# Two-layer hybrid diffusion backbone: GpSimd's low-part subtractions in parts of 256 columns

## The chip, the cores and the metric

The kernel runs on one core of a Trainium2 chip. The metric is the device time of one execution in microseconds (us). Before the change three runs gave a median of 2991.61 us (2990.83 to 2998.21).

## The reference

The input is a stream of 1024 latent tokens and 256 context tokens of width 1024, in float32. Two layers follow. Every sub-layer is modulated (a shift, a scale and a gate from a SiLU vector), and ends in a residual and a layer norm; each layer closes with a squared-ReLU MLP of inner width 4096.

```python
h  = x  * (1.0 + sc1)  + sh1          # modulated latents; context tokens alike (hc)
# layer 0: one projection feeds 4 retention heads and 4 gated-linear-attention heads,
# both bidirectional and chunked (64 tokens); context states start the latent scan
yc, ctx_states = retention_gla_mixer(hc, *prm, s0)
y, _ = retention_gla_mixer(h, *prm, ctx_states);  y = y @ ev_w_out
# layer 1: grouped-query attention, window +-128, a sink logit per head, axial rotary,
# latent queries also read all context keys
y = merge_heads(window_attention(q, k, v, k_c, v_c, sink)) @ od_w_out
x = layer_norm(ALPHA * x + g1 * y)                                  # both layers
x = layer_norm(ALPHA * x + g2 * (square(relu((x*(1+sc2)+sh2) @ w1)) @ w2))
```

## The kernel before, in words

**Three matmuls for one.** Every large product is made in a reduced float32 form (`F32R`). An operand is first cut in two: a high part, its rounded copy, and a low part, `operand - high`. Then `mm3` (L240 to L243) accumulates three matmuls per 128-deep step k in PSUM: weight high by activation high (L241), weight high by activation low (L242), weight low by activation high (L243). So each weight tile and each activation tile needs one copy and one subtraction.

**Who cuts the weights.** `wsplit` (L224) loads a weight tile of 128x1024 into one of three `raw` buffers, lets ScalarE copy the high part (L229) and lets one engine subtract the low part (L230). That engine is GpSimd unless the caller names another. 260 weight tiles pass through it; 210 subtractions are on GpSimd and 50 on VectorE. In the layer-0 mixer stage the generator `srcs` lets u odd go to VectorE and u even to GpSimd, and `wnext` holds three tiles ahead of the one in use. `load_wv` (L541) cuts eight value weights the same way, five of them on GpSimd (L546).

**Who cuts the activations.** `split` (L233) makes the high part on VectorE (L237) or ScalarE (L235), the low part (L238) on the engine that is named. `h_steps` (L345) works through the eight k of a modulated tile in pairs of 128x512 (two k of 256 tokens): ScalarE scales and shifts, then `split`, with the low part in turn on VectorE and on GpSimd. In the first stage the low part of the third token chunk (128x1024, two k of 512 tokens) is GpSimd's too. Two subtractions of the layer-0 mixer's outputs are written out by hand and do not go through `split`: L985 (eight on GpSimd, 128x1024) and L981 (two on GpSimd, 128x512).

**The stages in order of time.** First projections of layer 0 with their modulation (to about 165 us); the scan states (to about 350 us); the layer-0 mixer, five pairs of 128-token tiles, in which projections, the output projection and layer norms of neighbouring pairs are woven into the scan by credit (`slot`, to about 740 us); the MLP of layer 0 (to about 1690 us); the attention's projections (to about 1860 us); attention with its output projection (to about 2255 us); the MLP of layer 1. In the MLPs `load(b+1)` asks for four weight tiles one block ahead of their use, and the pool `wg` has five `w` buffers.

**What orders the work.** The code is written in the wanted order. A scheduler places each engine's instructions, tracks which columns of a tile an instruction writes and reads, and puts in the semaphore waits; each engine then runs its own queue strictly in that order. GpSimd's queue also carries the scaling at the end of each layer norm (`acc`, L714), a scaling of the gates (L807), small copies that release DMAs, and some DMA issues.

Other names in the text: VectorE (DVE) adds a projection's output to the residual at L734 (`w_out_steps`) and L1040 (MLP), masks the scores of the gated-linear heads into `Pg` at L928, multiplies the gate tile `g` at L978, keeps the scan states `S` at L898, L900 and L902, subtracts and scales in the layer norm at L690 and L708, and squares the ReLU output `r` at L1025. L943 is the TensorE matmul that reads `Pg`; L664 sums for a layer norm. L1193 transposes the rotated keys or queries `kr`, which L1187 writes.

Of the kernel before, what the change touches and what calls it, by code (L numbers as in the profile page):

```python
# [9 lines left out]
F32 = mybir.dt.float32  # L10
# [4 lines left out]
ALU = mybir.AluOpType  # L15
# [19 lines left out]
def backbone(ctx: ExitStack, tc: tile.TileContext, xT, cin, wmod, bmod, lng, lnb, w1, w2,  # L35
# [9 lines left out]
    V, S, G, TE, SY = nc.vector, nc.scalar, nc.gpsimd, nc.tensor, nc.sync  # L45
# [11 lines left out]
    def nm(s):  # L57
        uid[0] += 1
        return f"{s}_{uid[0]}"
# [164 lines left out]
    def wsplit(pool, src, eng=None):  # L224
        raw = rawp.tile([P, 1024], F32, tag="raw", name=nm("raw"))
        SY.dma_start(raw, src)
        both = pool.tile([P, 2, 1024], F32R, tag="w", name=nm("w"))
        hi, lo = both[:, 0, :], both[:, 1, :]
        S.copy(hi, raw)  # L229
        (eng or G).tensor_tensor(lo, raw, hi.bitcast(F32), ALU.subtract)  # L230
        return hi, lo

    def split(hi, lo, src, lo_eng=None, hi_eng=None):  # L233
        if hi_eng is S:
            S.copy(hi, src)  # L235
        else:
            V.tensor_copy(hi, src)  # L237
        (lo_eng or V).tensor_tensor(lo, src, hi.bitcast(F32), ALU.subtract)  # L238

    def mm3(pt, wh, wl, xh, xl, start, stop):  # L240
        TE.matmul(pt, lhsT=wh, rhs=xh, start=start, stop=False)  # L241
# [107 lines left out]
    def h_steps(src, l, idx, j, hh, hl, tp, tag, nb=1, hi_eng=None, los=(V, G)):  # L349

        n = src.shape[2]
        for k2 in range(KT // 2):
            tmp = tp.tile([P, 2, 256], F32, tag=tag, name=nm("hf"), bufs=nb)
            for i in range(2):
                k = 2 * k2 + i
                S.activation(tmp[:, i, :n], src[:, k, :], AF.Identity, scale=osc[:, l, idx, k, j:j + 1],
                             bias=mod[:, l, 3 * idx, k, j:j + 1])
            split(hh[:, 2 * k2:2 * k2 + 2, :], hl[:, 2 * k2:2 * k2 + 2, :], tmp[:, :, :n], los[k2 % 2], hi_eng)
            yield
# [3 lines left out]
    with es_b1:  # L363
# [6 lines left out]
        lwh = b1.tile([P, 256], F32R, tag="lwh", name="lwh")  # L370
        lwl = b1.tile([P, 256], F32R, tag="lwl", name="lwl")
        split(lwh, lwl, lw)
        w0 = wsplit(wp, wfm[0])
        pus, pls = [pX() for _ in range(3)], [pX(), pY(), pY()]

# [8 lines left out]
        for q in range(4):  # L384
            first_mods(q, raws)
            x_ = xs
            if q < 3:
                raws = first_load(q + 1)
                xs = first_x(q + 1)
            for a in range(2):  # L390
                k = 2 * q + a
                for j, c0, c1 in ((1, 0, 256), (0, 256, T)):
                    S.activation(x_[:, a, c0:c1], x_[:, a, c0:c1], AF.Identity, scale=osc[:, 0, 0, k, j:j + 1],
                                 bias=mod[:, 0, 0, k, j:j + 1])
            for ci, (c0, N) in enumerate(CH):
                split(h1[ci][0][:, 2 * q:2 * q + 2, :], h1[ci][1][:, 2 * q:2 * q + 2, :], x_[:, :, c0:c0 + N],
                      G if ci == 2 else V)
            if q > 0:
                first_proj(q - 1)
# [60 lines left out]
        def unit_loop(*uf):  # L460
            wus = [wsplit(wp, wfm[u]) for u, _ in uf]
            for ci in range(3) if len(uf) == 1 else (2, 1, 0):
                c0, N = CH[ci]
                for wu, (_, fn) in zip(wus, uf):
                    pt = pX()
                    proj(pt, wu, h1, ci)
                    fn(pt, ci, N, c0)
# [60 lines left out]
    with pool(name="b2", bufs=1) as b2:  # L528
# [11 lines left out]
        def load_wv(k):  # L540
            raw = rawp.tile([P, 1024], F32, tag="raw", name=nm("raw"))  # L541
            SY.dma_start(raw, wv[k])
            hi = b2.tile([P, 1024], F32R, tag=f"wvh{k}", name=f"wvh{k}")
            lo = b2.tile([P, 1024], F32R, tag=f"wvl{k}", name=f"wvl{k}")
            S.copy(hi, raw)
            (V if k > 2 and k % 2 else G).tensor_tensor(lo, raw, hi.bitcast(F32), ALU.subtract)  # L546
            wvh.append(hi)
            wvl.append(lo)

# [18 lines left out]
        for k in range(3):  # L568
            load_wv(k)
        x0 = load_x(0, 1)  # L570
        for k in range(3, KT):
            load_wv(k)
        Scur = new_S()
        G.memset(Scur[64:128, 1:3], 0.0)
        for oi, t in enumerate(order):
# [6 lines left out]
            for hf, k in [(hf, k) for k in range(KT) for hf in range(2)] if oi == 0 else [(hf, k) for hf in range(2) for k in range(KT)]:  # L582
                sl = slice(hf * 512, hf * 512 + 512)
# [140 lines left out]
    def w_out_steps(y, wsrc, wp, acc, l, j, pW, engs=(None, None), wnext=None):  # L724

        n = acc.shape[2]
        yh, yl = y
        for u in range(KT):
            wh, wl = [w.rearrange("p (k m) -> p k m", k=KT) for w in (wnext() if wnext else wsplit(wp, wsrc[u], engs[u % 2]))]
            pt = pW()  # L730
            for k in range(KT):
                xh, xl = [y_[k // 4][:, k % 4, :] if isinstance(y_, list) else y_[:, k, :] for y_ in (yh, yl)]
                mm3(pt[:, :n], wh[:, k, :], wl[:, k, :], xh, xl, k == 0, k == KT - 1)
            V.scalar_tensor_tensor(acc[:, u, :], pt[:, :n], gta[:, l, 0, u, j:j + 1], acc[:, u, :],  # L734
                                   op0=ALU.mult, op1=ALU.add)
            yield
# [15 lines left out]
    with pool(name="b3", bufs=1) as b3:  # L752
# [99 lines left out]
        for tp_ in range(NT // 2):  # L852
# [118 lines left out]
            for i in range(2):  # L971
                sl = slice(i * P, (i + 1) * P)
# [238 lines left out]
    for grp in range(3):  # L1211
# [19 lines left out]
        for i in range(4):  # L1231
            src = wkv[i] if grp == 0 else wq[4 * (grp - 1) + i]
            wu.append(wsplit(wg, src, V if i % 2 else G))
        for t in range(0 if grp == 0 else 2, NT):
# [14 lines left out]
            n = t - 2  # L1249
# [315 lines left out]
```

## Time and profile before

| | before |
|---|---|
| median of 3 runs | 2991.61 us |
| the profiled execution | 2999.63 us, span 2997.8 us |
| TensorE (PE) busy | 2886.7 us, 96% of the span |
| VectorE (DVE) busy | 1618.5 us, 54% |
| ScalarE (ACT) busy | 982.1 us, 33% |
| GpSimd (POOL) busy | 811.2 us, 27% |
| mean granted TensorE clock | 0.986 |

The profile names an instruction by its source line, engine and operation, then `out<-in` by tile names with buffer numbers left out. "x210" is a count. A group's row gives its busy time and the mean of one in ns, and behind the bar the idle time of the engine before these instructions with what released it. In the view of waits a row gives who waited for whom, the total in us, how often, and the longest. A row of the timeline gives the start in us, the duration in us (of all merged instructions where the count is over 1), and in brackets the idle time before it. A row of a source line gives minimum, median and maximum in ns. A stage's row gives busy time and counts per engine, then the granted TensorE clock.

### The profile page before, as it was taken

The numbers are of one execution on the slowest core, as the hardware profiler recorded it, in microseconds if no ns is written. First come the engines' busy times: TensorE is split into PE (matmuls) and PEld (weight loads), VectorE is DVE, ScalarE is ACT, GpSimd is POOL, SyncE is SP. The second block draws the span as 40 slices with busy tenths as digits, with TensorE's granted clock in tenths as the row PEclk, the third lists the DMA queues.
The fourth block names the chain that finished last, engine by engine and source line by source line (L and its number), as shares of the span: only waits on it lengthen the run. The fifth ranks groups of instructions, "written<-read, shape, count | busy, mean of one in ns | idle before, by whom it ended". The sixth has DMA issues, their size and how long they took to land. (4 is left out here: it accounts for less than half of the span.)

```text
span 2997.8 us, 42313 instructions
## 1 busy us (share of the span) xinstructions
PE 2886.7 (96%) x17204; PEld 2389.1 (80%) x17204; DVE 1618.5 (54%) x2709; ACT 982.1 (33%) x1630; POOL 811.2 (27%) x610
## 2 busy tenths in 40 slices
PE   7989998999999999999999999999999999999997
PEld 4866788888888888888888777677678888888886
DVE  3754467777765544444534554666775343433346
ACT  4533344443311111111112532656653111122113
POOL 3120144455311111111111432234343222122111
PEclk9999999999999999999999999999999999999999
DMA  7378576663122222122210385122221111111111
GB/s 256 113 224 251 179 245 202 204 204 124 55 69 71 71 70 71 57 74 85 67 43 8 97 214 162 45 80 89 64 86 42 57 57 44 41 57 56 36 36 57
DMA packets 168354, 304.45 MB, mean 102 GB/s; under 512 B 13504, under 2 KB 98752, under 8 KB 167648
## 3 DMA queue, kind: packets, MB, share of 16 engines
q1 hardware_dynamic: 149744, 272.91, 28.4%
q0 software_dynamic: 6480, 16.26, 2.0%
q10 hardware_dynamic: 11936, 12.59, 1.5%
q8 instruction: 135, 2.21, 0.3%
q14 instruction: 59, 0.48, 0.1%
HBM read 257.67 MB, written 44.04 MB: 101 GB/s over the span
## 5 line engine op out<-in xcount | busy, mean ns | idle before, releaser
L230 POOL TENSOR_TENSOR w<-raw,w 128x1024 fp32r<-128x1024 f32 x210 | 508.7, 2430 | 1644.5 <-ACT w L229 1602.4
L1040 DVE SCALAR_TENSOR_TENSOR acc<-k,gta,acc 128x512 f32<-128x512 f32 (+1 forms) x704 | 441.2, 648 | 567.4 <-PE k L243 559.9
L242 PE MATMUL k<-hl,w 128*128 128x256 f32 (+1 forms) x1632 | 554.5, 340 | 5.9 <-POOL hl L238 4.6
L241 PE MATMUL k<-hh,w 128*128 128x256 f32 (+1 forms) x1632 | 554.4, 340 | 5.1 <-DVE hh L237 3.4
L243 PE MATMUL k<-hh,w 128*128 128x256 f32 (+1 forms) x1632 | 551.1, 338 | 0.2 <-POOL w L230 0.2
L229 ACT CAST w<-raw 128x1024 fp32r<-128x1024 f32 x260 | 269.4, 1048 | 768.8 <-PE k L243 450.8
L241 PE MATMUL k<-uh,w 128*128 128x512 f32 (+1 forms) x1408 | 498.8, 354 | 9.2 <-DVE acc L1040 8.8
L242 PE MATMUL k<-ul,w 128*128 128x512 f32 (+1 forms) x1408 | 495.5, 352 | 0.0
L243 PE MATMUL k<-uh,w 128*128 128x512 f32 (+1 forms) x1408 | 494.7, 351 | 0.0
L241 PEld LDWEIGHTS k<-hh,w 128*128 128x128 f32 x1632 | 312.4, 192 | 49.9 <-issue 11.4
L242 PEld LDWEIGHTS k<-hl,w 128*128 128x128 f32 x1632 | 312.5, 192 | 45.5 <-POOL hl L238 6.1
L243 PEld LDWEIGHTS k<-hh,w 128*128 128x128 f32 x1632 | 312.9, 192 | 33.1 <-issue 1.7
L241 PEld LDWEIGHTS k<-uh,w 128*128 128x128 f32 x1408 | 266.9, 190 | 54.3 <-DVE acc L1040 16.6
L242 PEld LDWEIGHTS k<-ul,w 128*128 128x128 f32 x1408 | 266.9, 190 | 36.1 <-issue 0.8
L243 PEld LDWEIGHTS k<-uh,w 128*128 128x128 f32 x1408 | 266.8, 189 | 36.2 <-issue 0.8
L1022 ACT ACTIVATE r<-k 128x512 f32<-128x512 f32 (+1 forms) x176 | 90.6, 515 | 611.9 <-PE k L243 611.6
L241 PE MATMUL k<-yh,w 128*128 128x256 f32 (+1 forms) x544 | 183.7, 338 | 7.7 <-DVE acc L734 7.7
L159 DVE SCALAR_TENSOR_TENSOR k<-raw,cs,k 128x256 f32<-128x256 f32 (+1 forms) x168 | 96.5, 575 | 161.4 <-DMA raw<-in_wmod 159.3
L242 PE MATMUL k<-yl,w 128*128 128x256 f32 (+1 forms) x544 | 180.9, 333 | 0.0
L243 PE MATMUL k<-yh,w 128*128 128x256 f32 (+1 forms) x544 | 180.3, 331 | 0.0
L1025 DVE TENSOR_TENSOR r<-r 128x1024 f32<-128x1024 f32 (+1 forms) x88 | 110.0, 1250 | 68.9 <-ACT uh L1024 68.8
L714 POOL TENSOR_SCALAR acc<-acc,lg_t,lb_t 128x256 f32<-128x256 f32 x124 | 102.0, 834 | 117.1 <-DVE acc L708 47.5
(308 smaller groups left out, 4530.1 us busy)
## 6 DMA issues: line engine op xcount, KB each, us to landing
raw<-in_w SPq DMA_DIRECT2D x128, 512.0 KB, 3.3
raw<-in_wo SPq DMA_DIRECT2D x72, 512.0 KB, 3.6
raw<-in_wmod SPq DMA_DIRECT2D x128, 256.0 KB, 2.8
raw<-in_wfm SPq DMA_DIRECT2D x48, 512.0 KB, 5.5
raw<-in_wmod SPq DMA_DIRECT2D x32, 512.0 KB, 4.4
kt<-kd SPq DMA_DIRECT2D x20, 512.0 KB, 5.8
qt<-qT POOLq DMA_DIRECT2D x32, 256.0 KB, 4.3
qT<-qT ACTq DMA_DIRECT2D x30, 256.0 KB, 3.7
```

Source lines behind the costliest of these rows:

```text
L159: V.scalar_tensor_tensor(dst, src, cs[:, k + a, j:j + 1], dst, op0=ALU.mult, op1=ALU.add)
L229: S.copy(hi, raw)
L230: (eng or G).tensor_tensor(lo, raw, hi.bitcast(F32), ALU.subtract)
L241: TE.matmul(pt, lhsT=wh, rhs=xh, start=start, stop=False)
L242: TE.matmul(pt, lhsT=wh, rhs=xl, start=False, stop=False)
L243: TE.matmul(pt, lhsT=wl, rhs=xh, start=False, stop=stop)
L714: G.tensor_scalar(acc[:, k, :], acc[:, k, :], lg_t[:, l, s, k:k + 1], lb_t[:, l, s, k:k + 1], op0=ALU.mult, op1=ALU.add)
L1022: S.activation(rf[:, i, :n], pts[i][:, :n], AF.Relu)
L1025: V.tensor_tensor(rf[:, :, :n], rf[:, :, :n], rf[:, :, :n], ALU.mult)
L1040: V.scalar_tensor_tensor(a_, pt[:, :n], gta[:, l, 1, m, cj(ci):cj(ci) + 1], a_, op0=ALU.mult, op1=ALU.add)
```

## The change: parts of 256 columns

A new helper `low` subtracts in slices. On GpSimd the last dimension is cut every 256 columns; on any other engine one instruction covers it all, as before. `wsplit` and `load_wv` call it, so a 128x1024 weight tile takes four GpSimd instructions in place of one. `split` calls it for GpSimd on tiles with two k, once for each k: 128x512 becomes two instructions of 128x256, and 128x1024 (the first stage) becomes four. L985 and L981 are left as they are. What is computed is the same.

```diff
-        (eng or G).tensor_tensor(lo, raw, hi.bitcast(F32), ALU.subtract)
+        low(eng or G, lo, raw, hi)
         return hi, lo
+
+    def low(eng, lo, src, hi):
+
+        n = lo.shape[-1]
+        for o in range(0, n, 256 if eng is G else n):
+            sl = slice(o, o + (256 if eng is G else n))
+            eng.tensor_tensor(lo[..., sl], src[..., sl], hi[..., sl].bitcast(F32), ALU.subtract)
 
     def split(hi, lo, src, lo_eng=None, hi_eng=None):
...
-        (lo_eng or V).tensor_tensor(lo, src, hi.bitcast(F32), ALU.subtract)
+        if lo_eng is G and len(lo.shape) == 3 and lo.shape[1] == 2:
+            for i in range(2):
+                low(G, lo[:, i, :], src[:, i, :], hi[:, i, :])
+        else:
+            (lo_eng or V).tensor_tensor(lo, src, hi.bitcast(F32), ALU.subtract)
...
-            (V if k > 2 and k % 2 else G).tensor_tensor(lo, raw, hi.bitcast(F32), ALU.subtract)
+            low(V if k > 2 and k % 2 else G, lo, raw, hi)
```

All instructions of the program come out in nearly the order they had; two places show what differs. The first is GpSimd's queue in the layer-0 mixer, at the turn from one pair of tiles to the next (about 513 to 527 us in the trace of before). `hl` is an activation's low part, `w` a weight tile, `acc` the residual stream in its layer norm. Before:

```order
L238 TENSOR_TENSOR hl_4453<-hf_4459,hh_4452 128x512
L230 TENSOR_TENSOR w_4398<-raw_4396,w_4398 128x1024
L238 TENSOR_TENSOR hl_4453<-hf_4469,hh_4452 128x512
L230 TENSOR_TENSOR w_4549<-raw_4547,w_4549 128x1024
L714 TENSOR_SCALAR acc_370_2836<-acc_370_2836,lg_t,lb_t 128x256 x8
L230 TENSOR_TENSOR w_4639<-raw_4637,w_4639 128x1024
```

After, the same place (the new lines shift the numbers: `low` is L238 there, the scaling L725):

```order
L238 TENSOR_TENSOR hl_4564<-hf_4570,hh_4563 128x256 x2
L238 TENSOR_TENSOR w_4506<-raw_4504,w_4506 128x256 x4
L238 TENSOR_TENSOR hl_4564<-hf_4581,hh_4563 128x256 x2
L238 TENSOR_TENSOR w_4662<-raw_4660,w_4662 128x256 x4
L725 TENSOR_SCALAR acc_370_2887<-acc_370_2887,lg_t,lb_t 128x256 x8
L238 TENSOR_TENSOR w_4755<-raw_4753,w_4755 128x256 x4
```

No row has changed its place; each subtraction has become two or four rows in a row, with nothing of another kind between its parts.

The second place is TensorE's queue where the mixer stage begins (about 353 us), with the waits on semaphores in brackets: the first projection, three matmuls for each k. Before:

```order
L241 MATMUL k_402_2904<-hh_2862,w_2886 128x256 [waits DVE_49]
L242 MATMUL k_402_2904<-hl_2863,w_2886 128x256 [waits Pool_49]
L243 MATMUL k_402_2904<-hh_2862,w_2886 128x256
L241 MATMUL k_402_2904<-hh_2862,w_2886 128x256
L242 MATMUL k_402_2904<-hl_2863,w_2886 128x256
L243 MATMUL k_402_2904<-hh_2862,w_2886 128x256
```

After (L241 to L243 are L252 to L254 there):

```order
L252 MATMUL k_402_2963<-hh_2913,w_2939 128x256 [waits DVE_49]
L253 MATMUL k_402_2963<-hl_2914,w_2939 128x256 [waits Pool_49]
L254 MATMUL k_402_2963<-hh_2913,w_2939 128x256
L252 MATMUL k_402_2963<-hh_2913,w_2939 128x256
L253 MATMUL k_402_2963<-hl_2914,w_2939 128x256 [waits Pool_49]
L254 MATMUL k_402_2963<-hh_2913,w_2939 128x256
```

The order is the same. Where one wait on GpSimd covered both k of a pair, each k now waits for its own part. Weight tiles gain waits in the same manner: TensorE's queue has 667 waits on GpSimd in place of 240.

## The prediction

> **What bounds the kernel now.** The profile's page came first:
>
> ```profile
> PE 2886.7 (96%) x17204; PEld 2389.1 (80%) x17204; DVE 1618.5 (54%) x2709; ACT 982.1 (33%) x1630; POOL 811.2 (27%) x610
> ```
>
> TensorE sets the end: 2886.7 of 2997.8 us. The change adds no matmul and takes none away, so it can only act on the 111 us in which TensorE stands still, and on its clock. Busy times and the granted clock by stage say where that lies:
>
> ```profile
> 395.30:402.20 6.90, 6.90 (x34) 6.90 (x34) 2.16 (x3) 1.53 (x2) 0.00 (x0) 0.51 0.76 282
> 470.40:477.30 6.90, 6.90 (x35) 6.90 (x35) 4.84 (x11) 0.60 (x1) 0.00 (x0) 0.51 0.56 173
> 525.00:528.50 3.50, 2.88 (x13) 2.88 (x14) 3.50 (x7) 1.04 (x1) 3.50 (x6) 0.51 0.89 282
> 254.90:261.70 6.80, 5.07 (x41) 4.10 (x42) 6.74 (x14) 1.21 (x2) 0.31 (x1) 1.00 0.71 232
> 520.00:533.00 13.00, 9.85 (x74) 9.65 (x73) 11.88 (x10) 5.17 (x9) 12.75 (x11) 0.87 0.35 110
> 800.00:1650.00 850.00, 845.06 (x4603) 730.03 (x4602) 418.25 (x678) 157.33 (x220) 142.37 (x65) 1.00 0.20 64
> ```
>
> In the layer-0 MLP (800 to 1650) TensorE is busy 845.06 of 850 us at full clock, and GpSimd 142.37: nothing done to GpSimd moves that stage. In the mixer stage (520 to 533) TensorE works 9.85 of 13 us while DVE works 11.88 and GpSimd 12.75. The first three rows are stretches in which the granted clock was 0.51, so each us of them is worth half a us of work. The view of waits names what TensorE stood for:
>
> ```profile
> PE k L241 <- DVE acc L1040: 8.8, 15, 1.9
> ...
> PE k L241 <- DVE acc L734: 7.7, 2, 4.6
> ...
> PE k L189 <- DVE acc L690: 6.0, 3, 2.3
> PE k L242 <- POOL hl L238: 4.6, 4, 2.2
> ...
> PE pE L1193 <- DVE kr L1187: 3.6, 4, 1.7
> PE k L943 <- DVE Pg L928: 3.4, 2, 1.8
> ...
> PE k L664 <- DVE acc L734: 1.9, 1, 1.9
> ```
>
> GpSimd itself is waited for in one row (4.6 us). The others wait for DVE. The rows by source line show that DVE is often held:
>
> ```profile
> L230 POOLq EVENT_SEMAPHORE  x223: 17/17/24567, 17.6 to 2897.7; - x112
> L230 POOL TENSOR_TENSOR w<-raw,w x210: 2347/2400/3442, 20.2 to 2924.6; 128x1024 fp32r<-128x1024 f32 x105
> L230 DVE TENSOR_TENSOR w<-raw,w x50: 1159/1218/3908, 243.1 to 2237.4; 128x1024 fp32r<-128x1024 f32 x50
> ```
>
> ```profile
> L238 DVE TENSOR_TENSOR hl<-hf,hh x36: 627/688/2868, 352.8 to 2281.6; 128x512 fp32r<-128x512 f32 x36
> L238 POOL TENSOR_TENSOR hl<-hf,hh x32: 1261/1292/2317, 354.0 to 2282.6; 128x512 fp32r<-128x512 f32 x32
> ```
>
> The same DVE subtraction takes 1218 ns in the middle and 3908 at worst; the excess is about one GpSimd subtraction of 2400. The timeline shows one such case, at 464 us:
>
> ```profile
> 464.07 2.63 POOL L230 TENSOR_TENSOR w<-raw,w 128x1024 fp32r<-128x1024 f32 x1 [5.67 <-ACT w L229]
> ...
> 464.38 3.41 DVE L230 TENSOR_TENSOR w<-raw,w 128x1024 fp32r<-128x1024 f32 x1
> ...
> 469.35 0.49 PE L943 MATMUL k<-Pg,vt 128*128 128x128 f32 x2 [1.78 <-DVE Pg L928]
> ```
>
> DVE's subtraction began 0.31 us behind GpSimd's, stood until GpSimd was through at 466.70, and then ran its 1.2 us. `Pg` came behind it on DVE, and TensorE waited 1.78 us for `Pg`. So one engine locks the other out for the length of an instruction. The question is whether it gives way at the end of each part. At the turn between pairs (DVE's rows, then GpSimd's, then TensorE's):
>
> ```profile
> 518.44 3.44 DVE L708 TENSOR_TENSOR acc<-acc,ln_s 128x1024 f32<-128x1024 f32 x2
> 521.81 3.37 DVE L230 TENSOR_TENSOR w<-raw,w 128x1024 fp32r<-128x1024 f32 x1
> ```
>
> ```profile
> 518.61 2.19 POOL L238 TENSOR_TENSOR hl<-hf,hh 128x512 fp32r<-128x512 f32 x1 [3.10 <-DVE hh L237]
> 520.77 3.32 POOL L230 TENSOR_TENSOR w<-raw,w 128x1024 fp32r<-128x1024 f32 x1
> ```
>
> ```profile
> 525.62 0.58 PE L241 MATMUL k<-yh,w 128*128 128x256 f32 x1 [3.15 <-DVE acc L734]
> ```
>
> GpSimd's `w` was queued right behind its `hl`, which ended at 520.80. Yet `w` took 3.32 us instead of 2.40: DVE's second L708 went in between, and then DVE's `w` had to let GpSimd's finish at 524.09. They take turns, instruction by instruction.
>
> **The change part by part.**
>
> *Price of a part.* From 512 to 1024 columns GpSimd's median grows by 2400 - 1292 = 1108 ns, 2.16 ns a column, which leaves 184 ns fixed. 256 columns are then 0.74 us. A weight tile costs 4 x 0.74 = 2.95 us (+0.55), a pair of k 1.48 (+0.18). Over 215 weight tiles, 36 pairs and four first-stage tiles that is 118 + 7 + 2 = 127 us more on GpSimd, 811 to about 938. In the MLPs it lies beside TensorE. The GPSIMD Engine Reference of the Trainium skill (Instruction dispatch) puts the wrapper's cost at tens of cycles an instruction; by that, with an estimate of 50 cycles, or 0.04 us, the added work would be near 30 us and the cost term below nearly nil. The trace's two medians speak for 184 ns, and I use them.
>
> *What DVE gets back.* A DVE instruction that meets GpSimd waits at most one part, 0.74 us, instead of up to 2.4. Place by place:
> - `Pg`, 3.4 us in two waits. At 464 the first part, with its own 0.23 us of delay (2.63 - 2.40), ends at about 465.04; DVE's `w` waits 0.66 instead of 2.19: 1.5 of 1.78 saved. The other wait (1.6) has the same shape; half, 0.8. Together 2.3.
> - `acc` L734, 7.7 us in two waits (3.15 and 4.6), at two turns of the same pattern. The first L708 meets the end of a part instead of waiting for all of `hl` (0.5 saved), and DVE's `w` waits about 0.74 instead of 3.37 - 1.22 = 2.15 (1.4 saved): 1.9 each, 3.8.
> - L664 behind L734, 1.9 us, here:
>
> ```profile
> 2250.42 2.73 DVE L238 TENSOR_TENSOR yl<-hf,yh 128x512 fp32r<-128x512 f32 x1
> ...
> 2253.60 0.62 PE L664 MATMUL k<-acc,ones 128*32 128x256 f32 x2 [1.88 <-DVE acc L734]
> ```
>
>  DVE's low part took 2.73 us against 0.69; with one part's wait at most it takes 1.43. 1.3 saved.
> - L1193 behind `kr`: of 3.6 us I count 0.4. L1040: 8.8 us in 15 waits, of which only those count where L1025 or L238 was held just before; 1.4, bounded by 0 and 8.8.
> - The 6.0 us of L189 stay: they lie behind the hand-written L985, which is not cut.
>
> Together 9.2 us. Behind each stall another can be late (DVE's next instruction, a sum in PSUM), so I carry four fifths: **7.4 us**.
>
> *The clock.* The stretches at 0.51 behind the `Pg` waits (395 and 470, 6.9 us each) and the turn at 525 (3.5 us) lost half of 17.3 us, 8.6. Not every stall brings one: from 254.9 to 261.7 TensorE was idle 1.73 of 6.8 us at clock 1.00. A stall of 0.25 us should bring none, one of 0.8 or 1.3 may. I take one stretch of 6.9 away: **3.5 us**, between 0 and 8.6. The page TensorE: Matmul & The Clock Gate of the Trainium skill (Why this matters for your kernels) asks only that idle gaps stay below about 3 us; by that rule the 1.78 us wait would have cost no clock and this term would be nil, but the row at 470.4 right behind it shows 0.51.
>
> *What it costs on the path.* TensorE's 4.6 us for GpSimd's `hl`: the first k now comes after 0.74 us instead of 1.29, the second after 1.48, or later if DVE goes in between. Four waits, +0.5 or -0.5 each. ScalarE also gets its `hf` buffer back 0.2 us later each time. I put **1.5 us** on it (-2 to +4). The 427 added waits on TensorE's queue are met long before they are reached, as weights are cut three tiles or a block ahead; I take 0. A met wait is 17 ns at least on GpSimd's queue, so 7 us is the upper end.
>
> Sum: -7.4 - 3.5 + 1.5 = -9.4 us. The profiled execution took 2999.63 us (its span and 1.8 around it), 8.0 above the median of the three runs; from the median, 2991.61 - 9.4 = **2982 us**, from the profiled execution 2990.
>
> **The rivals.**
>
> *The stalls move instead of going.* Each DVE delay that ends is replaced by the next late thing, the clock windows fall as before, and half of the 7.4 us is left: 2991.6 - 3.7 + 1.5, about 2989. For it: in 520 to 533 DVE is busy 11.88 of 13, so it stays late with no lock at all. Against: the 464 case, where DVE's wait is the whole stall.
>
> *GpSimd's own queue becomes late (slower).* At a turn GpSimd was busy 12.75 of 13 us. Its queue there holds two `hl` and three `w`, now 2 x 0.18 + 3 x 0.55 = 2.0 us longer, and behind them the layer norm's L714 and the uncut `yl`, for which DVE and TensorE wait. Four turns make 8 us, and two more half-speed stretches of 3.5 us lose another 3.5: +11.5, about 3003. It decides once GpSimd's added time at a turn is over what DVE wins there (1.9 us); the two are close. Against: 0.92 of the 3.32 us of `w` are waits for DVE, which shorten too.
>
> *The parts run as one block.* If GpSimd never lets DVE in between two parts, a held DVE instruction waits up to 2.95 us instead of 2.40, 0.5 more at about ten places, plus 1.5: +6.5, 2998. The GPSIMD Engine Reference (Instruction dispatch) points that way: each of its cores starts the next instruction as soon as its own share of the last is done, so the engine need not be free at a part's end. Against it, DVE's L708 at 520.8. For it, one case at the edge of attention: DVE's subtraction began while GpSimd was in a short L714, and GpSimd's next subtraction passed it:
>
> ```profile
> 2237.40 3.91 DVE L230 TENSOR_TENSOR w<-raw,w 128x1024 fp32r<-128x1024 f32 x1 [0.60 <-ACT w L229]
> ...
> 2237.82 2.40 POOL L230 TENSOR_TENSOR w<-raw,w 128x1024 fp32r<-128x1024 f32 x1
> ```
>
> **How the numbers follow.** About 0.3% (9 us) is what a measurement of this kernel can tell from no change. The forecast (2982, faster by 0.32%) gets 0.48, the moved stalls 0.35, the block 0.05 (both within 9 us), the late queue 0.12. That is faster 0.48, same 0.40, slower 0.12. The range begins where all of the 9.2 us and the clock's 8.6 are won with 2 us at `hl`, 2972, and reaches over the moved stalls to the costs with nothing won, 4 us above the median, 2996. Most of the late queue lies outside.
>
> **What would show it.** In the changed profile: GpSimd's parts at about 0.74 us and its busy time near 940; DVE's L230 maximum near 2 us instead of 3.9; TensorE's waits behind `Pg` below 1.5 us in total, behind L734 near 5; fewer stretches at 0.51 in the mixer; the MLP unchanged. The prediction is wrong if DVE's maxima stay (parts run as a block), if TensorE's waits on `yl`, `hl` or L714's work grow by over 5 us (late queue), or if TensorE's matmuls in the MLP come slower (the added waits cost).

## The result

| kernel | median, us (runs) | ratio to before, with its interval | profiled execution, span |
|---|---|---|---|
| before, timed beside it | 2990.80 (9) | | 2999.63, 2997.8 |
| after | 3005.66 (9) | 1.0058 [1.0047, 1.0069] | 3008.61, 3006.8 |

The change makes the kernel slower by 0.58%, about 17 us by the ratio and 14.9 by the medians. The prediction had 2982 us and at most 2996. Of the runs below, one (parts in the layer-0 MLP alone) took 4543.76 us; it is in that kernel's median and in no ratio.

In the page of after, GpSimd works 952.0 us where 811.2 stood, and one part of 256 columns takes 742 ns in the middle (740 was worked out). The first row is from the page, the second from the rows by tile:

```profile
PE 2887.0 (96%) x17204; PEld 2386.0 (79%) x17204; DVE 1582.6 (53%) x2709; ACT 982.8 (33%) x1630; POOL 952.0 (32%) x1303
```

```profile
L238 POOL TENSOR_TENSOR w<-raw,w x840: 713/742/2344, 20.2 to 2935.6; 128x256 fp32r<-128x256 f32 x168
```

DVE's busy time falls by 35.9 us: it stands locked out for less. TensorE's waits are what decides. From the view of waits of after (who waits for whom, us in total, times, longest), the rows that answer to those of before:

```profile
PE k L252 <- DVE acc L1051: 15.8, 16, 2.0
PE k L252 <- DVE acc L745: 10.0, 4, 2.9
...
PE k L253 <- POOL hl L238: 3.7, 6, 1.4
...
PE pE L252 <- DVE acc L745: 3.0, 1, 3.0
...
PE pE L1204 <- DVE kr L1198: 2.1, 3, 1.6
PE k L954 <- DVE Pg L939: 0.8, 1, 0.8
PE k L675 <- DVE acc L745: 0.5, 1, 0.5
```

`Pg` (3.4 to 0.8), `kr` (3.6 to 2.1) and L675 (1.9 to 0.5) went down. Three rows went up: the MLP's residual L1051 from 8.8 to 15.8, the projection's residual L745 from 7.7 in two waits to 10.0 in four, and a new 3.0 for `pE` at the end of attention. The stage's row shows where the first of them stands:

```profile
800.00:1650.00 850.00, 839.93 (x4542) 723.85 (x4544) 406.92 (x664) 155.31 (x216) 168.72 (x228) 1.00 0.19 62
```

TensorE works 839.93 of 850 us in the layer-0 MLP, 845.06 before, and does 61 matmuls fewer in that time. Counted from the same matmul to the same matmul (numbers 4800 to 10000 of 17204), the MLP takes 947.9 us where it took 935.5. That is the stage in which the prediction expected nothing.

**One turn of the MLP, before and after.** DMA issues on SP's queue, GpSimd, DVE and TensorE where the next block's weights are cut. Before:

```profile
1160.87 2.68 SPq L226 DMA_DIRECT2D raw<-in_w  x2
1163.64 8.97 SPq L148 DMA_DIRECT2D raw<-in_wmod  x3
```

```profile
1158.44 4.75 POOL L230 TENSOR_TENSOR w<-raw,w 128x1024 fp32r<-128x1024 f32 x2 [25.36 <-ACT w L229]
```

```profile
1168.01 0.75 DVE L159 SCALAR_TENSOR_TENSOR k<-raw,cs,k 128x512 f32<-128x512 f32 x1 [5.70 <-DMA raw<-in_wmod]
```

```profile
1172.70 0.39 PE L241 MATMUL k<-uh,w 128*128 128x256 f32 x1 [1.03 <-DVE acc L1040]
```

After:

```profile
1164.36 3.11 SPq L226 DMA_DIRECT2D raw<-in_w  x2
1167.56 8.86 SPq L148 DMA_DIRECT2D raw<-in_wmod  x3
```

```profile
1161.50 5.62 POOL L238 TENSOR_TENSOR w<-raw,w 128x256 fp32r<-128x256 f32 x8 [23.95 <-ACT w L229]
```

```profile
1171.76 0.76 DVE L159 SCALAR_TENSOR_TENSOR k<-raw,cs,k 128x512 f32<-128x512 f32 x1 [6.51 <-DMA raw<-in_wmod]
...
1175.98 0.87 DVE L1051 SCALAR_TENSOR_TENSOR acc<-k,gta,acc 128x256 f32<-128x256 f32 x2
```

```profile
1176.51 0.39 PE L252 MATMUL k<-uh,w 128*128 128x256 f32 x1 [1.80 <-DVE acc L1051]
```

Two tiles take GpSimd 5.62 us where they took 4.75 (+0.87). A `raw` buffer is free when its low part is done. SP, which issues strictly in order, waits for that buffer with the next weight load at its head, and behind that load stands the one of `w_mod`. This is `mod_sums` (L148, L159), the modulation of the next layer, which is summed on DVE beside the MLP. From GpSimd's start to the issue of `w_mod` it is 5.20 us before and 6.06 after (+0.86). DVE stands at L159 for `w_mod` 0.81 us longer, with the residual L1051 queued behind it, and TensorE, whose next matmul needs the PSUM bank that L1051 empties, waits 0.77 us longer. Such turns come again until about 1293 us; some cost more and some nothing. Over the same matmuls of the whole MLP TensorE stands idle 18.4 us where it stood 10.3, and half-speed stretches lose 5.1 us where they lost 1.7 (after has them at 752, 1118 and 1674 us, before at 1668). Together that is 11.5 of the 12.4 us. The prediction saw TensorE busy for 845 of 850 us and a GpSimd that is idle most of the time, and did not follow what the end of GpSimd's instruction sets free.

### The profile page after: what moved, and what is told of

Read it like the earlier page. It is cut to its first block, busy times and chain, and to the rows that moved or that the text cites. A ratio compares the mean times of both kernels' runs of the same rounds, so it can differ in the third digit from the quotient of the medians.

```text
span 3006.8 us, 43081 instructions
## 1 busy us (share of the span) xinstructions
PE 2887.0 (96%) x17204; PEld 2386.0 (79%) x17204; DVE 1582.6 (53%) x2709; ACT 982.8 (33%) x1630; POOL 952.0 (32%) x1303
## 5 line engine op out<-in xcount | busy, mean ns | idle before, releaser
L238 POOL TENSOR_TENSOR w<-raw,w 128x256 fp32r<-128x256 f32 x840 | 637.4, 793 | 1545.9 <-ACT w L229 1447.9
L1051 DVE SCALAR_TENSOR_TENSOR acc<-k,gta,acc 128x512 f32<-128x512 f32 (+1 forms) x704 | 442.5, 649 | 569.4 <-PE k L254 568.4
L252 PE MATMUL k<-hh,w 128*128 128x256 f32 (+1 forms) x1632 | 554.7, 340 | 4.8 <-DVE hh L244 4.0
L254 PE MATMUL k<-hh,w 128*128 128x256 f32 (+1 forms) x1632 | 551.4, 338 | 0.0
L252 PE MATMUL k<-uh,w 128*128 128x512 f32 (+1 forms) x1408 | 499.7, 355 | 16.5 <-DVE acc L1051 15.8
L254 PE MATMUL k<-uh,w 128*128 128x512 f32 (+1 forms) x1408 | 495.4, 352 | 0.0
L252 PEld LDWEIGHTS k<-hh,w 128*128 128x128 f32 x1632 | 312.4, 192 | 50.5 <-issue 12.6
L254 PEld LDWEIGHTS k<-hh,w 128*128 128x128 f32 x1632 | 312.6, 192 | 32.7 <-issue 1.7
L252 PEld LDWEIGHTS k<-uh,w 128*128 128x128 f32 x1408 | 267.5, 190 | 62.2 <-DVE acc L1051 25.3
L254 PEld LDWEIGHTS k<-uh,w 128*128 128x128 f32 x1408 | 267.6, 190 | 36.4 <-POOL hl L238 0.8
L252 PE MATMUL k<-yh,w 128*128 128x256 f32 (+1 forms) x544 | 182.1, 335 | 10.0 <-DVE acc L745 10.0
L159 DVE SCALAR_TENSOR_TENSOR k<-raw,cs,k 128x256 f32<-128x256 f32 (+1 forms) x168 | 96.7, 576 | 175.5 <-DMA raw<-in_wmod 173.5
L254 PE MATMUL k<-yh,w 128*128 128x256 f32 (+1 forms) x544 | 179.1, 329 | 0.0
L1036 DVE TENSOR_TENSOR r<-r 128x1024 f32<-128x1024 f32 (+1 forms) x88 | 101.3, 1151 | 69.5 <-ACT uh L1035 69.4
L725 POOL TENSOR_SCALAR acc<-acc,lg_t,lb_t 128x256 f32<-128x256 f32 x124 | 98.2, 804 | 112.7 <-DVE acc L719 44.2
```

Source lines behind the costliest of these rows:

```text
L159: V.scalar_tensor_tensor(dst, src, cs[:, k + a, j:j + 1], dst, op0=ALU.mult, op1=ALU.add)
L238: eng.tensor_tensor(lo[..., sl], src[..., sl], hi[..., sl].bitcast(F32), ALU.subtract)
L254: TE.matmul(pt, lhsT=wl, rhs=xh, start=False, stop=stop)
L725: G.tensor_scalar(acc[:, k, :], acc[:, k, :], lg_t[:, l, s, k:k + 1], lb_t[:, l, s, k:k + 1], op0=ALU.mult, op1=ALU.add)
L1036: V.tensor_tensor(rf[:, :, :n], rf[:, :, :n], rf[:, :, :n], ALU.mult)
L1051: V.scalar_tensor_tensor(a_, pt[:, :n], gta[:, l, 1, m, cj(ci):cj(ci) + 1], a_, op0=ALU.mult, op1=ALU.add)
```

## The experiments

Where an experiment cuts in some places only, the number 256 in `low` and `split` becomes a variable; 1024 leaves subtractions whole. "Until the MLP" and the like mean the lines at which it is set. Added lines shift the numbers: L1040 of before (the residual in the MLP) is L1041 to L1053 in the other kernels, and L734 (the residual behind a projection) is L745 to L749.

```diff
+    part = [256]
...
-        for o in range(0, n, 256 if eng is G else n):
-            sl = slice(o, o + (256 if eng is G else n))
+        c = min(part[0], n) if eng is G else n
+        for o in range(0, n, c):
+            sl = slice(o, o + c)
...
-        if lo_eng is G and len(lo.shape) == 3 and lo.shape[1] == 2:
+        if lo_eng is G and len(lo.shape) == 3 and lo.shape[1] == 2 and part[0] == 256:
```

All results in one table. The ratio is to runs of before on the same chip; it is not the quotient of the medians and differs from it by up to 0.11% (the medians of before lie between 2988.2 and 2990.8 us in the sets). Mixer and MLP are one trace's times in us between the same matmuls (1840 to 4800, 4800 to 10000).

| what is cut | median, us (runs) | ratio, interval | mixer | MLP of layer 0 |
|---|---|---|---|---|
| nothing (before) | 2990.80 (9) | | 394.6 | 935.5 |
| all (after) | 3005.66 (9) | 1.0058 [1.0047, 1.0069] | 389.9 | 947.9 |
| until the MLP | 2992.98 (12) | 1.0011 [0.9998, 1.0024] | 390.2 | 933.5 |
| that MLP alone | 3002.00 (12) | 1.0047 [1.0032, 1.0063] | 388.5 | 946.8 |
| behind that MLP alone | 2995.05 (10) | 1.0023 [1.0012, 1.0034] | 387.1 | 933.0 |
| all but that MLP | 2998.48 (12) | 1.0020 [1.0004, 1.0036] | 390.1 | 932.4 |
| whole, and lengthened | 3029.16 (5) | 1.0127 [1.0108, 1.0146] | 395.5 | 958.4 |
| weights in 512 | 2992.62 (12) | 1.0010 [0.9996, 1.0023] | 388.9 | 934.4 |
| all; MLP loads on GpSimd's queue | 2998.06 (12) | 1.0029 [1.0014, 1.0043] | 391.7 | 935.3 |
| nothing; MLP loads on GpSimd's queue | 2986.40 (12) | 0.9987 [0.9975, 1.0000] | 389.0 | 928.4 |
| activations alone | 2995.19 (12) | 1.0020 [1.0009, 1.0032] | 388.9 | 935.1 |
| first-stage activations alone | 2991.13 (12) | 1.0010 [0.9997, 1.0023] | 388.8 | 935.1 |
| until the MLP, first-stage activations whole | 2990.08 (12) | 1.0008 [0.9995, 1.0021] | 389.0 | 933.7 |
| the same; MLP loads on GpSimd's queue | 2985.62 (11) | 0.9991 [0.9981, 1.0001] | 391.2 | 928.7 |
| nothing; `S<-st` on ScalarE's queue | 2993.61 (11) | 1.0008 [0.9995, 1.0021] | 389.4 | 932.8 |
| until the MLP (as above); `S<-st` on ScalarE's queue | 2987.14 (12) | 0.9987 [0.9974, 1.0001] | 383.0 | 933.2 |
| the same; both moves | 2979.43 (7) | 0.9961 [0.9948, 0.9973] | 381.2 | 930.6 |

### In which stage is it lost?

Parts until the MLP, and in that MLP alone:

```diff
+    part[0] = 1024
     es_h = ExitStack()
```

```diff
-    part = [256]
+    part = [1024]
...
+    part[0] = 256
     es_h = ExitStack()
...
+    part[0] = 1024
     qTd = [[dr.tile([2, 2, 64, 4, P], F32, tag=f"qT{n}_{i}", name=f"qT{n}_{i}") for i in range(2)] for n in range(8)]
```

Expected of the first:

> GpSimd's low parts are cut at 256 columns up to the end of the layer-0 mixer, whole from the layer-0 MLP on. Queue theory (in the MLP a longer weight subtraction frees its raw buffer later, SP's queue and with it the next load of w_mod comes later, DVE waits for that load and TensorE for DVE): the mixer keeps what the changed kernel won (TensorE about 5 us ahead of the kernel before when the MLP starts), the MLP's waits of TensorE behind L1040 fall back from 15.8 to about 9 us, and the time is 5 to 10 us below the kernel before. Contention theory (more GpSimd parts cost everywhere): the time lies between the two kernels, 3 to 8 us above the kernel before.

Expected of the second:

> Cut at 256 columns in the layer-0 MLP alone, whole elsewhere. Queue theory: nearly all that the MLP lost is there, +6 to +12 us against the kernel before, with TensorE's waits behind L1040 near 15 us in place of 8.8. Rival (the loss comes from DVE held by the trains of parts outside the MLP, at the turns of the mixer and at the end of attention): within 3 us of the kernel before.

The MLP alone gives 0.47% of the 0.58% (some 14 us, a little over the 6 to 12 expected), and its stage takes 946.8 us, near the 947.9 of after; without it the stage is back at 933.5. That half of the theory held. The other half missed: without the MLP's loss there is no gain left, 1.0011 with an interval that holds 1.

The complement, all but that MLP:

```diff
+    part[0] = 1024
     es_h = ExitStack()
...
+    part[0] = 256
     qTd = [[dr.tile([2, 2, 64, 4, P], F32, tag=f"qT{n}_{i}", name=f"qT{n}_{i}") for i in range(2)] for n in range(8)]
```

> All parts as in the change, except in the layer-0 MLP, where weights are subtracted whole. Theory: the loss of that stage goes (935 us), and what is left is the sum of the other stages: 0.58% less the 0.47% that parts in that stage alone cost, so 0.1%, 2991 us (2987 to 2995). Rival: attention behind the MLP loses as much as the mixer wins or more (399 us against 394.5, GpSimd's trains at 2244 us): 2995 to 2999, as with the other queue (0.29%).

The MLP stage is 932.4, as the theory said. The median lies in the rival's range; the interval of the ratio is too wide to tell the two apart. Whether something is lost behind the MLP as well is seen with parts there alone:

```diff
-    part = [256]
+    part = [1024]
...
+    part[0] = 256
     qTd = [[dr.tile([2, 2, 64, 4, P], F32, tag=f"qT{n}_{i}", name=f"qT{n}_{i}") for i in range(2)] for n in range(8)]
```

> Parts of 256 only from behind the layer-0 MLP on (attention, its edge, the last MLP). Train theory: at about 2235 us DVE's low part of a weight is passed over by eight GpSimd parts and takes 7.1 us instead of 3.9, TensorE waits 3.0 us for pE behind L734 and a half-speed stretch of 3.4 or 6.8 us follows, as in the three traces with parts of 256 there; attention 398 to 399 us instead of 394.5; 2993 us in all (2990 to 2996). Rival, that it needs what the mixer or the MLP left behind: DVE's longest stays at 3.9, 394 to 395 us, 2987 to 2991.

The theory held in its main points: 1.0023, slower, and the train is there. GpSimd, DVE and TensorE of this kernel at the end of attention:

```profile
2235.66 5.59 POOL L240 TENSOR_TENSOR w<-raw,w 128x256 fp32r<-128x256 f32 x8
```

```profile
2235.24 7.10 DVE L240 TENSOR_TENSOR w<-raw,w 128x1024 fp32r<-128x1024 f32 x1 [0.59 <-ACT w L230]
2242.26 0.86 DVE L747 SCALAR_TENSOR_TENSOR acc<-pE,gta,acc 128x256 f32<-128x256 f32 x2
```

```profile
2242.87 0.55 PE L254 MATMUL pE<-yh,w 128*128 128x256 f32 x1 [3.00 <-DVE acc L747]
```

DVE's subtraction begins while GpSimd is in a short layer-norm instruction; then all eight parts of two tiles pass it, and it ends 1.1 us behind the last of them. Before, it took 3.91 us at this place: one whole tile passed it, and it got in between the two. In all four kernels with weight parts of 256 there, DVE took 7.1 us and TensorE waited 3.0. The place is not all of the 6.9 us that the timed runs show behind the MLP; attention takes 397.2 us in this trace (398 to 399 were expected), 394.7 in that of before, and the rest is not placed.

### Is it GpSimd's time, and does it go through SP's queue?

Subtractions whole again, each weight tile's first 176 columns subtracted a second time (that work is repeated, the output is the same):

```diff
+        if eng is None or eng is G:
+            G.tensor_tensor(lo[:, 0:176], raw[:, 0:176], hi[:, 0:176].bitcast(F32), ALU.subtract)
         return hi, lo
```

> The kernel before, with each whole weight subtraction on GpSimd followed by a second one that repeats its first 176 columns: about 0.55 us more of GpSimd for a tile, no parts. Queue theory: the time of GpSimd is what counts, so the layer-0 MLP loses as much as with parts (waits behind L1040 13 to 17 us), and as DVE gets nothing back in the mixer the whole is 12 to 25 us above the kernel before. Rival (parts themselves cost, by their waits on TensorE's queue or by locking DVE out one after the other): under 5 us above the kernel before.

No part and no change of order, and the MLP loses 22.9 us: it is GpSimd's time that counts, not the cutting. The whole is some 38 us above before by the ratio, more than the 12 to 25 expected. Two tiles take 4.76 + 1.10 = 5.86 us, more than with parts (5.62):

```profile
1168.90 4.76 POOL L230 TENSOR_TENSOR w<-raw,w 128x1024 fp32r<-128x1024 f32 x2 [23.86 <-ACT w L229]
1173.62 1.10 POOL L232 TENSOR_TENSOR w<-raw,w 128x176 fp32r<-128x176 f32 x2
```

The other direction, weights in parts of 512 (pairs of k are cut as in the change):

```diff
+    part = [512]
```

> Weights are cut into parts of 512 columns instead of 256; the pairs of k stay cut as in the change. By the trace a part of 512 takes 1.29 us, so a tile takes 2.58, 0.18 more than whole, where the change added 0.55. Queue theory (raw buffers come free later, so the load of w_mod behind them on SP comes later): the layer-0 MLP loses about a third of the 12.4 us, some 4 us, its stage 938 to 941; with a like share of the rest, 2994 us (2990 to 2998). If the loss there came from the number of instructions or the added semaphores, half of it: 942 and more. If only trains of parts that pass over DVE matter, the MLP is as with 256 columns and DVE's longest wait is that of two parts, about 2.6 us.

Two tiles take 5.05 us, and the stage takes 934.4: not a third of the loss but none (932.4 to 935.5 in the nine traces with whole weights and the loads on SP). Two instructions a tile cost nothing that these traces can tell. TensorE's waits for the residual grow with GpSimd's time all the same. From the view of waits of 800 to 1650 us, in turn before, 512, after, and lengthened:

```profile
PE k L241 <- DVE acc L1040: 4.5, 10, 1.0
```

```profile
PE k L254 <- DVE acc L1053: 6.2, 10, 1.5
```

```profile
PE k L252 <- DVE acc L1051: 10.7, 12, 1.8
```

```profile
PE k L243 <- DVE acc L1042: 19.5, 16, 3.8
```

With 4.75, 5.05, 5.62 and 5.86 us for two tiles the waits are 4.5, 6.2, 10.7 and 19.5 us. A small addition costs little and the next one much: the path was near its limit before the change.

Now the queue. `wsplit` issues its loads on GpSimd's queue during this MLP, so that `w_mod` on SP stands behind none of them. In the changed kernel, and in the one before:

```diff
-        SY.dma_start(raw, src)
+        wq_[0].dma_start(raw, src)
...
+    wq_[0] = G
     es_h = ExitStack()
...
+    wq_[0] = SY
     qTd = [[dr.tile([2, 2, 64, 4, P], F32, tag=f"qT{n}_{i}", name=f"qT{n}_{i}") for i in range(2)] for n in range(8)]
```

> The changed kernel, with the weight loads of the layer-0 MLP issued from GpSimd's queue, so that SP's queue holds only the w_mod loads there. Queue theory: the w_mod loads no longer stand behind a raw buffer; TensorE's waits behind L1040 drop below the 8.8 us of the kernel before, and the time is 7 us or more below the changed kernel. Contention theory: the waits stay near 15 us, and the time stays within 3 us of the changed kernel.

> The kernel before, without any parts, with the weight loads of the layer-0 MLP issued on GpSimd's queue and not on SP's. Queue theory: w_mod's loads no longer stand behind a load that waits for GpSimd, so TensorE's 6.8 us behind L1040 in that stage shrink to about 3 and the stage takes 932 to 934 instead of 935.5; in all 2983 to 2988. Rival, that the other queue is worth nothing or costs something by itself (the issues lie in GpSimd's own order): the stage takes 935.5 or more and the whole 2988 to 2995; then the 12.6 us that the same move gave back to the changed kernel are all the loss that the parts had made.

The changed kernel gets 12.6 us of that stage back in the trace and half of its loss in time (0.58% to 0.29%). Its waits for the residual in 800 to 1660 us, and those of the kernel before with the same move:

```profile
PE k L253 <- DVE acc L1052: 3.8, 4, 1.5
```

```profile
PE k L242 <- DVE acc L1041: 3.9, 5, 1.9
```

Off SP's order, parts make no difference to these waits any more: same parts, same time on GpSimd, no added wait. The stage is still 6.9 us longer than that of the kernel before with the move (935.3 to 928.4), and all of that is lost where the mixer's last work and the MLP's first blocks meet: TensorE's lag behind that kernel changes by 6.9 us between 740 and 808 us and by less than 0.1 us from there to the MLP's end. Of the 6.9 us, 6.0 lie between 740 and 782: TensorE waits 2.44 us at 749.8 and 1.29 at 754.2 for a layer norm (the kernel before with the move waits 1.39 once), and a half-speed stretch of 6.8 us, which loses 3.4, begins at 750.4. Why the layer norm is late there was not tried. The kernel before also had something to win by the move: 928.4 us where nine traces have 932.4 to 935.5, and 0.13% in time, at the edge of its interval.

### What do the activations and the first stage do?

Only activations cut (`wsplit` and `load_wv` as before):

```diff
-        low(eng or G, lo, raw, hi)
+        (eng or G).tensor_tensor(lo, raw, hi.bitcast(F32), ALU.subtract)
...
-            low(V if k > 2 and k % 2 else G, lo, raw, hi)
+            (V if k > 2 and k % 2 else G).tensor_tensor(lo, raw, hi.bitcast(F32), ALU.subtract)
```

> Only the activations' subtractions are cut (pairs of k, first-stage tiles); all weights are whole. Theory: everything lost hangs on the weights (raw buffers in the MLP, trains of weight parts at 522, 601 and 2244 us), so this is as before or a little below, 2983 to 2990, MLP stage 935. Rival: the cut of the activations costs in the mixer and attention (a later hl, an hf buffer that comes free later): 2991 to 2996, with waits of TensorE for hl above the 4.6 us of before.

2995.19, a miss for the theory that all hangs on the weights. The rival's time fits, its sign does not: TensorE's waits for `hl` are 3.5 us, not above 4.6. In the first stage the trace is 5.2 us behind that of before (167.1 to 161.9), though in all it is no longer. There the granted clock was half for 13 us. The same is seen between two other kernels. The rows for 69 to 82 us of after, and of the kernel with parts until the MLP, which has the same instructions there:

```profile
69.00:82.00 13.00, 13.00 (x58) 9.29 (x58) 8.31 (x10) 12.38 (x13) 1.71 (x3) 1.00 0.33 118
```

```profile
69.00:82.00 13.00, 13.00 (x33) 8.09 (x34) 5.30 (x7) 8.79 (x10) 1.30 (x2) 0.50 0.29 96
```

By then four of six traces with those activations cut had the stretch, and none of four with them whole. Two kernels tested whether the cut brings it about: the first-stage activations cut alone, and parts until the MLP with those activations whole. The diff is the second one's; the first has 1024 and 256 exchanged.

```diff
+                part[0] = 1024
                 split(h1[ci][0][:, 2 * q:2 * q + 2, :], h1[ci][1][:, 2 * q:2 * q + 2, :], x_[:, :, c0:c0 + N],
                       G if ci == 2 else V)
+                part[0] = 256
```

> As before, except that the first-stage activations (the split of x_, four GpSimd subtractions in the whole program) are cut. Clock theory: the four traces with a first stage of 166 to 167 us instead of 161 to 162 all had these subtractions cut and a stretch of 13.7 us at half speed from 68 or 69 us on, while none of the four traces with them whole had it. So eight small instructions bring it about: a stage of 166 to 167 us, a stretch near 69 us, and 2994 us in all (2992 to 2997), 5 above before, as with the activations alone cut. Rival, that the stretch is chance in that execution: no such stretch or no loss in time, 2987 to 2991.

> Parts as in the change up to the layer-0 MLP, but the first-stage activations whole; everything from that MLP on whole. Clock theory: against the run with parts until the MLP (2993.0) the half-speed stretch at 69 us goes and 5 us with it: first stage 161 to 162, 2987 us in all (2983 to 2990), and what parts win in the mixer is all that is left, 2 us or nothing. Rival: the mixer's own gain is nil and the stage's clock was chance, 2991 to 2995. The forecast's 9.4 us of gain would need 2980.

The theory fell. The first kernel, cut there, has a first stage of 161.0 us and no such stretch; the second, whole there, has 166.3 us and the stretch, as has the kernel with parts behind the MLP alone (167.1). Over all 17 traces seven have it, four of them with the cut and three without. It comes and goes between executions and is worth some 5 us of the spread. Why activations alone are 0.20% slower stays open.

### Where did the mixer's gain go?

In the mixer, six traces with weight parts of 256 there take 390.4 us on average (389.0 to 391.7), and six with whole weights 390.6 (387.1 to 395.5). The prediction's `Pg`, L734 and clock terms, some 8 of its 10.9 us of gain, lie there; that gain is not to be seen, though `Pg` is 0.4 to 1.2 us in the traces with parts of 256 and 3.0 to 4.2 in five of the six without. The kernel with parts in the mixer alone, in the view of waits:

```profile
PE k L254 <- DVE acc L749: 10.2, 4, 2.9
...
PE k L958 <- DVE Pg L943: 1.2, 2, 0.8
```

Where before had two waits for the residual (3.15 us at 525, 4.59 at 603), this kernel has four, two of them 2.92 us at places where before had none. In the changed kernel SP, DVE and TensorE ahead of the first of these two:

```profile
525.17 1.41 SPq L226 DMA_DIRECT2D raw<-in_wfm  x3
526.63 0.42 SPq L895 DMA_DIRECT2D S<-st  x1
```

```profile
527.59 0.75 DVE L926 TENSOR_TENSOR Pr<-k,Dm 128x256 f32<-128x256 f32 x2
534.35 0.35 DVE L909 SCALAR_TENSOR_TENSOR S<-S,decs,S 64x128 f32<-64x128 f32 x1 [6.01 <-DMA S<-st]
```

```profile
537.33 0.40 PE L252 MATMUL k<-yh,w 128*128 128x256 f32 x1 [2.92 <-DVE acc L745]
```

DVE is early now and stands 6.01 us (4.59 before) for the scan states `S<-st`. SP issued them at 526.63, behind weight loads of which one had stood 6.8 us for GpSimd's `w`, whose four parts ended at 525.15. The gain seems to be given back to SP's order again.

At the turn itself the lock is not relieved. GpSimd's and DVE's rows of after there:

```profile
522.36 2.79 POOL L238 TENSOR_TENSOR w<-raw,w 128x256 fp32r<-128x256 f32 x4
```

```profile
522.89 3.33 DVE L238 TENSOR_TENSOR w<-raw,w 128x1024 fp32r<-128x1024 f32 x1 [3.63 <-ACT w L229]
```

All four parts of the tile go ahead of DVE's `w`, which takes 3.33 us here and 3.62 at the second turn (601 us), where before had 3.37 and 3.36. The prediction had it wait for one part. What got shorter is DVE's time elsewhere: its busy time in the mixer is 284.1 us in before (350 to 744 us) and 272.9 in after (348 to 737).

The test of SP's order: that one load on ScalarE's queue, without parts and with parts in the mixer.

```diff
-                    SY.dma_start(St, st[t])
+                    S.dma_start(St, st[t])
```

> The kernel before with one edit: the scan states' load S<-st (L884) is issued on ScalarE's queue instead of SP's, so that it no longer stands behind weight loads that wait for GpSimd. If that order holds the mixer: TensorE's two waits behind L734 (7.4 to 8.8 us in all traces with whole weights) shrink by 1 to 3 us, the mixer takes 384 to 388 us, in all 2986 to 2990. Rival, that the load's 7.2 us of transfer or DVE's own work is what is late: waits and stage as before, 2989 to 2993.

> The run with parts in the mixer alone (2990.1), with S<-st on ScalarE's queue. Theory for the lost mixer gain: DVE, with parts, comes 3.5 us earlier in sum to the scan step and waits for S<-st that SP issues late behind weight loads; the four waits behind L734's line (1.8, 2.9, 2.6, 2.9 us) are then set by it. So the two of 2.9 us fall below 1.5, the mixer takes 382 to 386 us instead of 389 to 391, in all 2983 to 2987, and the gain over the same move without parts is 2 us or more. Rival, that DVE's own queue sets them: four waits of 10 us as before, mixer 388 to 391, 2988 to 2992.

Without parts the move wins nothing in time (1.0008) and the mixer takes 389.4 us; with parts it takes 383.0, and the time goes from 2993.61 to 2987.14, 6.5 us (1.0008 to 0.9987, each within 0.0014), just clear of the two intervals taken together. The two waits of 2.92 us are gone. From the waits of the mixer, without parts and with:

```profile
PE k L241 <- DVE acc L734: 8.4, 2, 4.6
```

```profile
PE k L254 <- DVE acc L749: 2.6, 1, 2.6
```

So parts do win something in the mixer, some 6 us, once the next thing on SP's queue no longer sets DVE's time. The expectation for the kernel without parts (waits shorter by 1 to 3 us) missed: there DVE itself is late, and the load's place costs nothing.

### A version that beats both

Parts until the MLP, with the MLP's loads moved (`wq_`, as above), and with that and the states' load moved (`S.dma_start`, as above):

> The run with parts in the mixer alone, and the weight loads of the layer-0 MLP on GpSimd's queue with whole subtractions there. If the mixer's gain (2 us or nothing) and that of the other queue without parts (3 us) add up: first stage 161 to 162, MLP stage 928 to 930, 2984 us in all (2980 to 2987), the fastest of all. Rival: the mixer wins nothing, as with the other queue alone, 2986 to 2989.

> Parts until the layer-0 MLP (first-stage activations whole), S<-st on ScalarE's queue, and the layer-0 MLP's weight loads on GpSimd's queue with whole subtractions there. If both queues' findings hold, they add: mixer 383 to 385 us, MLP stage 928 to 930, 2982 us in all (2979 to 2985), 0.25% under the kernel before and the fastest of all versions. Rival, that the second move meets the first (the mixer's early weight tiles, DMA contention): as with one move alone, 2985 to 2989.

The first has the MLP stage that was expected (928.7 us), but 0.9991 is not told from 1. The second has 381.2 us in the mixer, 930.6 in the MLP and 2979.43 us in all, 0.9961 [0.9948, 0.9973]: 11 us under the kernel before, the only version that is clearly faster. The load of the states is again worth some 6 us or more beside parts (2985.62 to 2979.43; 0.9991 to 0.9961). The two places on SP's queue add up, as separate causes would.

## Why the prediction was wrong, point by point

**The step that failed** is "In the MLPs it lies beside TensorE", with "nothing done to GpSimd moves that stage". Busy shares of that stage were read, not who waits for GpSimd's end. With parts in that MLP alone the kernel lost 0.47%, and with its loads off SP's queue the parts add nothing to the waits for the residual (3.8 us against 3.9). The trace before the change shows the path: between 800 and 1750 us SP's queue stood 306.6 us with a weight load for GpSimd's `w`, and DVE stood 158.8 us for `w_mod`:

```profile
SPq L226 <- POOL w L230: 306.6, 53, 27.4
```

```profile
DVE k L159 <- DMA raw<-in_wmod: 158.8, 53, 8.6
```

**The price of a part** was right: 742 ns for 740. GpSimd is busy 952.0 us in place of 938; some parts stand longer than others, and their mean is 793 ns.

**`Pg`, 2.3 us**: right, 2.6 (3.4 to 0.8). **L664, 1.3 us**: right in size there (1.9 to 0.5), but just ahead of it the train of eight parts put 3.0. **`kr`, 0.4 us**: too small, 1.5 (3.6 to 2.1). **L1040, 1.4 us**: wrong in sign, 8.8 to 15.8; this is the failed step again. **L734, 3.8 us**: wrong in sign as the kernel stands (7.7 to 10.0). Its working failed too, as DVE's `w` at the two turns waited for four parts and not for one. With `S<-st` on another queue the waits do fall (8.4 to 2.6). The text had asked what is late next only by a factor of four fifths; it was nearly all.

**The clock, 3.5 us**: the stretches at 395 and 470 are gone in after, but others came. In the mixer 14.8 us are lost to half speed on average in the six traces with whole weights and 14.0 in the six with parts of 256: 0.8 us.

**Cost at `hl`, 1.5 us**: its row went down, 4.6 to 3.7. **Added waits on TensorE's queue, 0**: not told apart by itself; with 512 columns two instructions a tile cost the MLP nothing that shows.

**The rivals.** The moved stalls describe the mixer well: its gain is gone. The late queue forecast the sign and nearly the time (3003), for the wrong queue and place: not GpSimd's at the mixer's turns but SP's, which waits for GpSimd, in the MLP. The parts as one block hold at few places. Yet the prediction's sign for it came, as DVE's longest low part of a weight went from 3.9 us to 7.1, where near 2 was forecast. In most meetings DVE gets in behind one part (its longest squaring, L1036, is 1.68 us, that of L1025 was 2.10); at the mixer's two turns it stands behind four, and at 2244 us behind eight.

**The sum** as the runs give it: parts until the MLP +0.11%, in it +0.47%, behind it +0.23%, each within 0.16. That is 0.81 against 0.58 for all together; the difference is within these intervals taken together, and no finer account is shown.

## What to carry to other kernels

An engine with idle time still holds a buffer until its instruction ends: follow that end to the queue that waits for the buffer, and to everything queued behind that wait, before you price a longer instruction at nothing. A load that waits for a buffer should not share an in-order queue with a load that another engine needs soon. When a lock or stall is relieved, look at what the freed engine waits for next, and move that too; here parts in the mixer and the move of one load were worth nothing that could be measured apart, and some 6 us beside each other.

## What the runs showed of the hardware

**A waiting DVE instruction can be passed over many times.** At the end of attention eight GpSimd instructions in a row (5.59 us) went ahead of a DVE subtraction that had begun before them, with parts of 256 in all four traces; with parts of 512 it took 4.06 us at that place, with whole tiles 3.91. At the mixer's turns four went ahead (3.33 and 3.62 us for 1.22). The Trainium skill, SBUF — State Buffer (SBUF: two separate sides), says that of a GpSimd instruction and a VectorE one with two inputs in SBUF, whichever starts first has the shared ports for its whole instruction. These rows agree for one instruction; what happens at an instruction's end, where one waits and the other has more, the runs show to go both ways, and what decides it is open.

**A fixed time for each GpSimd instruction.** Four parts against one whole subtraction (4 x 742 against 2400 ns) leave 189 ns for each added instruction.

**The clock's stretch of 13 us in the first stage** came in 7 of 17 profiled executions, with the activations cut or whole, and is worth some 5 us.
